# Feed-forward columns of both streams in one matmul, paired heads in part C, and a new order of the mixer's projections

## The chip, the core and the metric

The kernel runs on one core of a Trainium2 chip. Its engines are TensorE (PE; its weight loads are listed apart as PEld), VectorE (DVE), ScalarE (ACT), GpSimd (POOL) and SyncE (SP, which issues most loads). The metric is the device time of one execution in microseconds. Before the change the median of three runs is 2468.3 us (2467.7 to 2470.83).

## The reference, cut to what matters

Two transformer blocks of two layers each, in float32, 256 positions of width 1024. The first block (retention, stick-breaking attention, feed-forward) is left as it was but for buffers. The second carries two streams, the latents `x` and the context `h`, through the same weights:

```python
for l in range(DEPTH):                      # DEPTH = 2
    x = ffn_sublayer(x, mod_x, 0, *f0)      # swiglu, 1024 -> 2816 -> 1024
    h = ffn_sublayer(h, mod_h, 0, *f0)      # the same weights
    ax, ah = adaln_in(x, ...), adaln_in(h, ...)
    uv_x, qb_x, qc_x, kb_x, vb_x, kc_x, vc_x = split(ax @ w_in[l])
    # h: all of them in layer 0, only kb, vb, kc, vc in layer 1
    o_a = chunk_gmlp(uv_x, ...)             # part A: gelu, norm, 128 x 128 mix, times u
    o_b = diff_attention_latent(...)        # part B: 4 heads, two softmaxes of 64-wide keys each
    o_c = swa_latent(qc_x, kc_x, vc_x, kc_h, vc_h, sink)   # part C: 4 heads over 2 key-value heads
    x = adaln_out(x, concat(o_a, o_b, o_c) @ w_out[l], ...)
    # h the same in layer 0; then both through the second feed-forward
    x = ffn_sublayer(x, mod_x, 2, *f1)      # h too, but not in the last layer
```

`mod_x` and `mod_h` are products of a conditioning vector with `w_mod`, which is 9 x 1024 columns a layer.

## The kernel before, in words

**Precision.** A weight tile arrives as float32 (`raw`, four slots) and is split by ACT and DVE into a high and a low part (`hl`, five slots; a "granule" is one such tile of 512 KB). Activations are split in the same way (`y`, `a`, `o`). A product is three float32r matmuls, high by high, high by low and low by high (`mm3`). Attention itself runs in plain float32, where the program has two PE instructions for each matmul: the trace counts both, the order counts one.

**Feed-forward (`ffn`, `col`, `row_units`).** The 2816 hidden columns are 22 tiles `j`. A column (`col`) makes gate and up of tile `j` for one stream: 2 x 8 x 3 = 48 matmuls of 256 moving columns (the stream's 256 tokens) into one PSUM bank, tile `mm_c`; then ACT takes silu, DVE multiplies, ACT and DVE split the result into `a`. A row unit multiplies two tiles of `a` with one granule of the down weights, 6 matmuls of 512 columns; four make a row. The context H adds its rows up in SBUF (`mm_r`, `fo`), the latents X keep theirs in four PSUM banks (`mm_f`). Both streams use one granule of weights, so H and X stay within five granules of each other; X has granules of its own for its last two columns and rows (`OWN_C`, `OWN_R`), and in the second feed-forward of layer 0 for its first four columns (`OWN_B`).

**Mixer (`attn2`).** Projections are two half units of 24 matmuls each (`half1`, `half2`; `vb` is `wide1`, `wide2`) in the order kb0, kb1, vb, kcvc, v, qb0, u, qb1, qc. Softmax work is a list of items, eight for part B (head, half of the queries) and eight for part C; a stream of its own (`sat`) issues scores (`at_s`), softmax, transposes (`at_t`), weighted values (`at_o` in B, `at_c` in C), two items ahead (`DIST`). A B item has two score matmuls on the two halves of the partitions (64 rows of keys each); a C item has one. Part A's mix is `gm` (`at_g`), B's norm `bapply` (`st_rb`). Then `w_out` in four pieces, 1, 2 (B), 0 (A), 3 (C), 96 matmuls `mm_f<-hl,o`.

**Order.** `run` is a planner: it holds the streams `sx` (X), `sh` (H), `sat`, `smod` (the sums of `w_mod`, DVE work of the lowest class) and `stot`, knows a cost for each kind of unit (`PE_NS`, `BANKS`) and writes one fixed order of instructions for each engine. PSUM is eight banks. At run time only semaphores decide when the next instruction of that order starts. All line numbers in the trace are the helper's (L205), so groups are told apart by tile names: `mm_y` is the transposed input of a stage, `mm_t` the modulation sums, `st_*` norms.

Of the kernel before, what the change touches and what calls it, by code (L numbers as in the profile page):

```python
# [11 lines left out]
F32 = mybir.dt.float32  # L12
# [35 lines left out]
GM_AT = 11  # L48
# [75 lines left out]
class Gran:  # L124


    def __init__(self, ap, kind):
# [9 lines left out]
PE_NS = {"col": 5760, "proj": 5760, "rope1": 5760, "half1": 2880, "half2": 2880, "wide1": 5450, "wide2": 5450, "row": 1365, "row_add": 1365, "row_last": 1365,  # L137
         "tr": 450, "total": 440, "put": 110, "rbc": 430, "start1": 30, "start2": 300, "r1": 650, "r2": 650, "r3": 430,
         "hstat": 1650, "happly": 3400, "s1": 650, "s2": 870, "s3": 650, "rope2": 860, "kcvc2": 650, "wst": 430,
         "sc2": 1730, "sc1": 870, "trp": 430, "avf": 1300, "avc": 860, "bst": 320, "gm": 1040, "bapply": 1740}  # L140
BANKS = {"row": 0, "wide1": 2, "wide2": 0, "row_add": 1, "row_last": 0, "half2": 0, "happly": 2, "sc2": 2, "bapply": 2}
CLASS = {"part": 3, "head": CLS_H, "tr": CLS_T, "post": CLS_P, "row_last": CLS_R, "row_add": CLS_A, "rfac": CLS_F,
         **{k: CLS_S for k in ("tv", "sc1", "sc2", "trp", "avf", "avc", "bst")}}
# [24 lines left out]
class Engine:  # L168
# [6 lines left out]
    def ns(self, op, args, kw):  # L175
# [283 lines left out]
def tile_two_blocks(ctx: ExitStack, tc, io, out):  # L459
# [31 lines left out]

    ytile = [None, None]
# [3 lines left out]
    u_half = {}  # L496
    ctab = [None, None]
# [119 lines left out]
    def pre_units(st, c, gain_of, shift_of, of, deps, hard=False):  # L617
# [58 lines left out]
        for i in range(4):  # L676
            u = st.add("tr", tr(i), deps=d)
            d = ()
        return u

    def pre_raw(gain_of, deps_lo, deps_hi, keep, at_start=False):
# [145 lines left out]
    def ffn(st, c, gg, gu, gd, mode, dep, pace, fac=None, by_token=True):  # L827
        abox = {}
        cols = {}

        def col(j):
            def fn():
# [4 lines left out]
                def tail():  # L837
# [16 lines left out]
                    if j == 0:  # L854
# [237 lines left out]
    def block1_layer(l, dep):  # L1092
# [103 lines left out]
        for h in range(4):  # L1196
# [49 lines left out]
        for h in range(4):  # L1246
# [70 lines left out]
        def sapply():  # L1317
# [78 lines left out]
    def mod_buf1():  # L1396
        a = wk.tile([P, 2, 2, D], F32, tag="y1", name="modacc")
        r = [wk.tile([P, 2, D], F32, tag=t, name="modraw") for t in ("k2", "v2")]
        return [t[:, x, :] for t in r for x in range(2)], [[a[:, x, 0, :], a[:, x, 1, :]] for x in range(2)]

    def mod_buf2():
# [3 lines left out]
        a2 = [wk.tile([P, D], F32, tag="wt", name="modacc", bufs=2) for _ in range(2)]  # L1405
# [3 lines left out]
    mod_units(0, 2, 4, pace0[23], [(u_s2, 0.0)], mod_buf1)  # L1409
# [17 lines left out]
    ORDER = [5, 6, 7, 8, 9, 2, 3, 4, 1, 0]  # L1427

    def attn2(l, c, main, gw, kv_only, dep, kvdeps):
# [159 lines left out]
        roped("kb0", 5, lambda: K2["k"][:, 0:2, half], 1.0, 1, [dep] + ([(totals[l, 8], 0.0)] if c == H else kvdeps[:1]))  # L1589
        roped("kb1", 6, lambda: K2["k"][:, 2:4, half], 1.0, 1)  # L1590
        vb()
        kcvc()
        if kv_only:
            flush()
            return None, ev
        if c == H or l == DEPTH - 1:
# [20 lines left out]
        uvv()  # L1617
        roped("qb0", 2, lambda: B["q"][:, 0:2, :], 0.125, 1)
        uvu()
        roped("qb1", 3, lambda: B["q"][:, 2:4, :], 0.125, 1)  # L1620

        roped("qc", 4, lambda: B["qc"], 0.125, 1)
        flush()

# [6 lines left out]
        def soft(todo, extra=None):  # L1631
# [3 lines left out]
            for p, ps, x in todo:  # L1635
                V.tensor_reduce(x[:, 0:1], ps[:, :n], axis=AX.X, op=ALU.max, negate=True)
                if extra is not None:
                    V.scalar_tensor_tensor(x[:, 0:1], extra, -1.0, x[:, 0:1], op0=ALU.mult, op1=ALU.min)
            yield A
            for p, ps, x in todo:  # L1640
# [337 lines left out]
```

## Time and profile before

| | us |
|---|---|
| median of three runs (lowest, highest) | 2468.3 (2467.7, 2470.83) |
| profiled execution, its own time | 2468.97 |
| its span, first to last instruction | 2467.1 |
| PE busy | 2409.6 (98%) |
| DVE, ACT, POOL busy | 1727.6, 1094.3, 99.3 |
| mean granted TensorE clock | 0.993 of full |

The span has four kinds of stretch: block one up to about 660 us, then for each layer of block two a feed-forward of both streams (660 to 1050 and 1700 to 2090 us), the mixers (1050 to 1335 and 2100 to 2257 us), and a second feed-forward (1290 to 1710 us for both streams, 2270 to 2460 us for X alone). "Busy" of PE counts an instruction from its start to its modelled end, neighbours overlapping; the time that a matmul takes of PE in a stream is read from the starts of neighbours or from the chain.

### The profile page before, as it was taken

To read this page: it belongs to the slowest core of one execution; us is meant where nothing else is said; L and a number is where in the kernel's file an instruction comes from. 1 tells how busy PE (TensorE), PEld (TensorE's weight loads), DVE (VectorE), ACT (ScalarE), POOL (GpSimd) and SP (SyncE) were. 2 spreads that over 40 slices of the span, in tenths; PEclk is the share of its full clock that TensorE was granted. 3 is DMA by queue.
4 is the path that set the end of the run, shared out by engine and by line. 5 is a ranking of instruction groups with operands and counts; after the bars stand their busy time and mean duration, and the time that the engine had idled before them with its cause. 6 is when DMAs were issued, how large, how long until landed. Compare 5 with 4: busy or idle time off the path is not lost.

```text
span 2467.1 us, 41782 instructions
## 1 busy us (share of the span) xinstructions
PE 2409.6 (98%) x16543; PEld 2211.5 (90%) x16543; DVE 1727.6 (70%) x3366; ACT 1094.3 (44%) x2331; POOL 99.3 (4%) x189
## 2 busy tenths in 40 slices
PE   8999999999999999999999999999999999997998
PEld 7999999999999999989669999999999999866997
DVE  5789667798789933756688994348998448486554
ACT  6654456545532222636465222236322226465443
POOL 1000000010011000000000100000110000000000
PEclk9999999999999999999999999999999999999999
DMA  7568655686667533522226652245675335322663
GB/s 228 165 209 263 179 168 158 191 267 194 205 188 210 167 98 90 178 88 84 62 94 205 214 180 86 86 120 188 206 213 154 95 87 181 93 86 78 190 193 120
DMA packets 455301, 386.26 MB, mean 157 GB/s; under 512 B 20512, under 2 KB 380260, under 8 KB 455104
## 3 DMA queue, kind: packets, MB, share of 16 engines
q1 hardware_dynamic: 431280, 299.67, 41.0%
q0 software_dynamic: 23648, 83.77, 10.7%
q8 instruction: 130, 2.13, 0.4%
q14 instruction: 67, 0.55, 0.1%
q10 hardware_dynamic: 176, 0.14, 0.0%
HBM read 382.43 MB, written 1.10 MB: 155 GB/s over the span
## 4 chain that ended last, share of the span: by engine, by line
PE 88%; DVE 8%; ACT 1%; DMA 1%; issue 1%; DVEq 0%; ACTq 0%
PE mm_c L205 57%; PE mm_f L205 17%; PE mm_r L205 6%; DVE hl L205 2%; PE at_s L205 2%; PE mm_t L205 1%; DVE res L205 1%; PE at_o L205 1%; DVE fo L205 1%; PE at_t L205 1%; DMA raw<-in_w_in_dram 1%; DVE t L205 1%; PE at_c L205 1%; PE st_rb L205 1%; DVE rs_t L205 1%
## 5 line engine op out<-in xcount | busy, mean ns | idle before, releaser
L205 PE MATMUL mm_c<-y,hl 128*128 128x256 f32 x11616 | 1436.4, 284 | 10.4 <-DVE y L205 7.5
L205 PEld LDWEIGHTS mm_c<-y,hl 128*128 128x128 f32 x11616 | 1418.8, 192 | 23.8 <-DVE y L205 8.8
L205 ACT CAST hl<-raw 128x512 fp32r<-128x512 f32 x1128 | 649.0, 619 | 814.5 <-PE mm_c L205 445.3
L205 DVE TENSOR_TENSOR hl<-raw,hl 128x512 fp32r<-128x512 f32 x1128 | 733.2, 685 | 339.4 <-ACT hl L205 338.3
L205 PE MATMUL mm_f<-hl,a 128*128 128x512 f32 x1584 | 381.5, 393 | 0.0
L205 PEld LDWEIGHTS mm_f<-hl,a 128*128 128x128 f32 x1584 | 291.5, 188 | 57.6
L205 DVE SCALAR_TENSOR_TENSOR modacc<-modraw,sc,modacc 128x1024 f32<-128x1024 f32 x252 | 311.6, 1277 | 0.0
L205 ACT ACTIVATE sg<-mm_c 128x256 f32<-128x256 f32 x154 | 58.6, 381 | 311.0 <-PE mm_c L205 307.5
L205 PE MATMUL mm_r<-hl,a 128*128 128x512 f32 x792 | 190.5, 392 | 0.0
L205 DVE TENSOR_TENSOR sg<-sg,mm_c 128x256 f32<-128x256 f32 x154 | 64.0, 416 | 154.0 <-ACT sg L205 153.2
L205 PEld LDWEIGHTS mm_r<-hl,a 128*128 128x128 f32 x792 | 145.2, 188 | 28.0
L205 PE MATMUL mm_f<-hl,o 128*128 128x512 f32 x480 | 119.3, 399 | 0.0
L1000 POOL DMA_DIRECT2D modraw<-in_w_mod_dram x144 | 77.3, 538 | 991.6 <-DVE modacc L205 625.8
L205 PE MATMUL mm_c<-hl,y 128*128 128x512 f32 (+1 forms) x528 | 108.7, 363 | 0.0
L205 PEld LDWEIGHTS mm_f<-hl,o 128*128 128x128 f32 x480 | 87.8, 189 | 23.1 <-issue 4.6
L205 PEld LDWEIGHTS mm_c<-hl,y 128*128 128x128 f32 x528 | 88.8, 189 | 14.7 <-issue 0.3
L205 DVE TENSOR_TENSOR fo<-fo,mm_r 128x512 f32<-128x512 f32 x120 | 81.6, 682 | 9.2 <-PE mm_r L205 8.5
L205 ACT CAST a<-sg 128x256 fp32r<-128x256 f32 x154 | 62.5, 406 | 30.1 <-DVE sg L205 30.0
L205 DVE TENSOR_TENSOR a<-sg,a 128x256 fp32r<-128x256 f32 x154 | 64.4, 418 | 8.5 <-ACT a L205 8.5
L205 DVE TENSOR_TENSOR gu<-mm_c,rfac 128x512 f32<-128x512 f32 x44 | 30.3, 688 | 48.7 <-PE mm_c L205 48.6
L205 DVE TENSOR_REDUCE sx<-at_s 128x1 f32<-128x512 f32 (+1 forms) x72 | 40.8, 596 | 26.3 <-PE at_s L205 25.7
L205 DVE TENSOR_REDUCE modt<-mm_t 128x4 f32<-128x512 f32 x72 | 49.2, 684 | 8.4 <-PE mm_t L205 8.2
(196 smaller groups left out, 1412.4 us busy)
## 6 DMA issues: line engine op xcount, KB each, us to landing
modraw<-in_w_mod_dram POOLq DMA_DIRECT2D x144, 512.0 KB, 4.7
raw<-in_ffn_w_down_dram SPq DMA_DIRECT2D x100, 512.0 KB, 4.4
raw<-in_ffn_w_gate_dram SPq DMA_DIRECT2D x98, 512.0 KB, 4.7
raw<-in_ffn_w_up_dram SPq DMA_DIRECT2D x98, 512.0 KB, 3.9
raw<-in_w_in_dram SPq DMA_DIRECT2D x92, 512.0 KB, 4.7
raw<-in_w_gate_dram SPq DMA_DIRECT2D x44, 512.0 KB, 4.9
raw<-in_w_up_dram SPq DMA_DIRECT2D x44, 512.0 KB, 5.1
raw<-in_w_down_dram SPq DMA_DIRECT2D x44, 512.0 KB, 4.9
```

The costliest lines, as they stand in the source:

```text
L205: return f(*args, **kw)
L1000: G.dma_start(M["raw"][g % len(M["raw"])], wm[k * P:(k + 1) * P, i * D:(i + 1) * D])
```

## The change

1. **Joint columns.** `yy` is one buffer for the inputs of both streams. In a joint column one matmul has as its moving operand both streams' 256 tokens, `yy[:, :, 0, k, :]`, two runs of 256 columns that lie apart; gate and up are units of 24 matmuls with 512 columns, a bank each. ACT and DVE do silu and product once for 512 columns and the split into `a` once for each stream. Tiles 2 to 19 are joint in the first feed-forward of each layer and 4 to 19 in the second one of layer 0: 18 + 18 + 16 = 52 columns. The first joint gate also waits for X's input, and an up waits for the X row that last read the slots of `a` which it writes.
2. **Part C in pairs.** Eight items become four (query group, half of the queries), each with both key-value heads: two score matmuls on the two halves of the partitions, two softmaxes, eight transposes; the weighted values go to both halves of the output partitions, alternating. The rows of `w_out` for part C are loaded in a matching order, as two transfers of 64 partitions for a granule.
3. **Order.** The projections come as kb0, kb1, qb0, vb, qb1, kcvc, qc, v, u (layer 0) and kb0, kb1, vb, qb0, qb1, kcvc, qc, v, u (layer 1), `gm` after all items, `w_out` in pieces 1, 2, 3, 0. Scores wait only for the keys they use.
4. **Buffers.** `wt` has four buffers; the modulation sums of block one use the buffers that block two's used; the scratch for DMAs from GpSimd is set to 8192.

```diff
+BA_AT = 9
-GM_AT = 11
+GM_AT = (12, 12)
-PE_NS = {... "wide2": 5450, "row": 1365, ...}
+PE_NS = {... "wide2": 5450, "joint": 5450, "row": 1365, ... "trp2": 870, ...}
...
+    yy = cpool.tile([P, 2, 2, KT, S], F32R, name="yy")
-                    ytile[c] = wk.tile([P, 2, KT, S], F32R, tag=f"y{c}", name=f"y{c}")
+                    ytile[c] = yy[:, c]
...
+        def both(j):
+            box = {}
+
+            def part(g, ps):
+                for k in range(KT):
+                    mm3(ps, wsl(g, 0, k, 0, P), wsl(g, 1, k, 0, P), yy[:, :, 0, k, :], yy[:, :, 1, k, :],
+                        k == 0, k == KT - 1)
+
+            def gate():
+                ps = mm_ps([P, 2, S], "mm_c")
+                part(gg[j], ps)
+
+                def tail():
+                    yield A
+                    box["sg"] = t2k([P, 2, S], "sg")
+                    A.activation(box["sg"], ps, AF.Silu)
+                return tail
+
+            def up():
+                ps = mm_ps([P, 2, S], "mm_c")
+                part(gu[j], ps)
+
+                def tail():
+                    yield V, ug
+                    sg = box["sg"]
+                    V.tensor_mul(sg, sg, ps)
+                    for x in (H, X):
+                        yield A
+                        a = joint[1]["a", x]
...
+                        hl = a["t"][:, j % 4]
+                        A.copy(hl[:, 0, :], sg[:, x, :])
+                        yield V
+                        V.tensor_sub(hl[:, 1, :], sg[:, x, :], hl[:, 0, :])
+                        a[j] = hl
+                return tail
+            ug = st.add("joint", gate, grans=[gg[j]], deps=dep if j == 0 else ())
+            cols[j] = joint[1][j] = st.add("joint", up, grans=[gu[j]])
...
         for j in range(NJ):
-            col(j)
+            if joint is None or j not in joint[0]:
+                col(j)
+            elif c == H:
+                both(j)
+            else:
+                cols[j] = joint[1][j]
+                if j == joint[0][0]:
+                    joint[1]["first"].deps += ((last_of[X], 0.0),)
             if j >= 3 and j % 2 == 1:
-                row(j // 2 - 1)
+                u = row(j // 2 - 1)
+                if joint and c == X and j + 1 in joint[0]:
+                    joint[1][j + 1].deps += ((u, 0.0),)
...
-    mod_units(0, 0, 2, pace0[1], [(u_s2, 0.0)], mod_buf1)
+    mod_units(0, 0, 2, pace0[1], [(u_s2, 0.0)], mod_buf2)
...
+    SEQ = ("kb0 kb1 qb0 vb qb1 kcvc qc v u".split(),
+           "kb0 kb1 vb qb0 qb1 kcvc qc v u".split())
...
-        for v in range(2):
-            for g in range(2):
-                for b in range(2):
-                    hh = v * 2 + g
-
-                    def sc(v=v, g=g, b=b, hh=hh):
-                        ps = at_ps([P, 512], "at_s")
-                        PE.matmul(ps[:, :n], B["qc"][v * 64:v * 64 + 64, g, b * P:(b + 1) * P],
+        for g in range(2):
+            for b in range(2):
+                def sc(g=g, b=b):
+                    pt = ptile()
+                    pss = [at_ps([P, 512], "at_s") for _ in range(2)]
+                    for v in range(2):
+                        PE.matmul(pss[v][:, :n], B["qc"][v * 64:v * 64 + 64, g, b * P:(b + 1) * P],
                                   K2["kc"][v * 64:v * 64 + 64, 0:n], start=True, stop=True)
...
+                def avc(g=g):
+                    ps = at_ps([P, 512], "at_c")
+                    for j in range(nk):
+                        for v in range(2):
+                            PE.matmul(ps[v * 64:v * 64 + 64, :S], K2["vc"][:, j, v * 64:v * 64 + 64],
+                                      B["wtc", g][v][:, j, :], start=(j == 0), stop=(j == nk - 1))
...
-            otile[c] = wk.tile([P, 2, KT, S], F32R, tag=f"y{c}", name=f"o{c}")
+            otile[c] = yy[:, H] if l == DEPTH - 1 else yy[:, c]
...
+        pieces = (1, 2, 3, 0) if GM_AT[l] >= 12 else (1, 2, 0, 3)
+        joints = [(range(n, NJ - OWN_C), {}) for n in (2, OWN_B)]
...
+    nc = _bacc.Bacc("TRN2", target_bir_lowering=False, num_devices=1,
+                     dynamic_dma_scratch_size=8192)
```

What stands on PE in the first feed-forward of layer 0, before (`y_6515` is H's input, `y_7250` X's; `a_7247` and `a_7420` are their hidden tiles):

```order
L205 MATMUL mm_f<-hl,a_7420 128x512 x18
L205 MATMUL mm_c<-y_6515,hl 128x256 x48
L205 MATMUL mm_r<-hl,a_7247 128x512 x12
L205 MATMUL mm_c<-y_7250,hl 128x256 x96
L205 MATMUL mm_r<-hl,a_7247 128x512 x12
L205 MATMUL mm_f<-hl,a_7420 128x512 x6
L205 MATMUL mm_c<-y_6515,hl 128x256 x48
L205 MATMUL mm_f<-hl,a_7420 128x512 x18
L205 MATMUL mm_c<-y_6515,hl 128x256 x48
L205 MATMUL mm_r<-hl,a_7247 128x512 x12
```

And after, over the same tiles (`a_7395` is X's):

```order
L206 MATMUL mm_f<-hl,a_7395 128x512 x24
L206 MATMUL mm_c<-yy,hl 128x512 x72
L206 MATMUL mm_r<-hl,a_7247 128x512 x24
L206 MATMUL mm_c<-yy,hl 128x512 x24
L206 MATMUL mm_f<-hl,a_7395 128x512 x24
L206 MATMUL mm_c<-yy,hl 128x512 x72
L206 MATMUL mm_r<-hl,a_7247 128x512 x24
L206 MATMUL mm_c<-yy,hl 128x512 x24
L206 MATMUL mm_f<-hl,a_7395 128x512 x24
```

Each `mm_c` of 48 with 256 columns for either stream has gone into a `mm_c` of 24 with 512 for both, and H's and X's rows stand whole between them.

PE around the first scores of X in the mixer of layer 1, before (`at_s<-k` scores of part B, `at_r` rotations):

```order
L205 MATMUL mm_c<-y_21857,hl 128x256 x96
L205 MATMUL at_r<-kr,tab_c_6411 128x256 x2
L205 MATMUL mm_c<-y_21857,hl 128x256 x24
L205 MATMUL at_s<-k_21693,at_21912 128x512 x4
L205 MATMUL mm_c<-y_21857,hl 128x256 x48
L205 MATMUL at_s<-k_21693,at_21912 128x512 x2
L205 MATMUL at_t<-cst,p 128x128 x4
L205 MATMUL at_s<-k_21693,at_21912 128x512 x2
L205 MATMUL mm_c<-y_21857,hl 128x256 x24
L205 MATMUL at_t<-cst,p 128x128 x4
```

And after:

```order
L206 MATMUL mm_c<-yy,hl 128x256 x144
L206 MATMUL at_t<-cst,kcr 128x128 x2
L206 MATMUL at_r<-kr,tab_c_6412 128x256 x2
L206 MATMUL mm_c<-yy,hl 128x256 x24
L206 MATMUL at_s<-k_19011,at_19237 128x512 x4
L206 MATMUL mm_c<-yy,hl 128x256 x24
L206 MATMUL at_r<-kr,tab_c_6412 128x256 x2
L206 MATMUL at_s<-k_19011,at_19237 128x512 x2
L206 MATMUL mm_c<-yy,hl 128x256 x24
L206 MATMUL at_t<-cst,p 128x128 x4
L206 MATMUL at_s<-k_19011,at_19237 128x512 x2
L206 MATMUL mm_c<-yy,hl 128x256 x24
```

The first scores stand further ahead: before, 48 + 24 projection matmuls of X are still to come behind them, now seven half units of 24.

PE at the end of the same mixer, before (`at_s<-kc` scores of part C, `at_c` its weighted values, `at_g` part A, `mm_f<-hl,o` the product with `w_out`):

```order
L205 MATMUL at_s<-kc,at_21912 128x512
L205 MATMUL at_t<-cst,p 128x128 x4
L205 MATMUL at_c<-wtc,vc 64x256 x4
L205 MATMUL at_s<-kc,at_21912 128x512
L205 MATMUL at_t<-cst,p 128x128 x4
L205 MATMUL mm_f<-hl,o_23026 128x512 x12
L205 MATMUL at_t<-cst,p 128x128 x4
L205 MATMUL at_c<-wtc,vc 64x256 x4
L205 MATMUL at_t<-cst,p 128x128 x4
L205 MATMUL mm_f<-hl,o_23026 128x512 x6
L205 MATMUL at_c<-wtc,vc 64x256 x4
L205 MATMUL mm_f<-hl,o_23026 128x512 x78
```

And after (`mm_f<-hl,yy` is that product, since `o` lies in `yy`):

```order
L206 MATMUL at_s<-kc,at_19237 128x512 x2
L206 MATMUL at_t<-cst,p 128x128 x8
L206 MATMUL st_h<-cst,bq 128x1 x2
L206 MATMUL st_rb<-cst,rs_t 128x128 x8
L206 MATMUL at_t<-cst,p 128x128 x8
L206 MATMUL at_c<-wtc,vc 64x256 x8
L206 MATMUL at_t<-cst,p 128x128 x8
L206 MATMUL at_c<-wtc,vc 64x256 x8
L206 MATMUL at_g<-ws,bt_19238 64x128 x8
L206 MATMUL mm_f<-hl,yy 128x512 x96
```

The scores of C stand in pairs, `at_c` in groups of eight, `at_g` behind all of them, and the whole product with `w_out` behind `at_g`, where 18 of its 96 matmuls stood between the last items.

## Rows read from the trace of the kernel before

**Rows 1.** The page, part 1: span and busy time of each engine.
```profile
span 2467.1 us, 41782 instructions
...
PE 2409.6 (98%) x16543; PEld 2211.5 (90%) x16543; DVE 1727.6 (70%) x3366; ACT 1094.3 (44%) x2331; POOL 99.3 (4%) x189
```

**Rows 2.** The page, part 4: chain that ended last, by engine.
```profile
PE 88%; DVE 8%; ACT 1%; DMA 1%; issue 1%; DVEq 0%; ACTq 0%
```

**Rows 3.** Chain of waits, 840 to 960 us: start us, length us, what.
```profile
848.11 5.47 PE mm_r L205 x24
...
897.90 11.51 PE mm_c L205 x96
```

**Rows 4.** Timeline of PE, layer 1 mixer: start us, us, what [idle before].
```profile
2178.66 1.13 PE L205 MATMUL at_s<-k,at 64*128 64x512 f32 x4
2179.72 0.66 PE L205 MATMUL at_t<-cst,p 128*128 128x128 f32 x4
...
2208.97 1.12 PE L205 MATMUL at_s<-kc,at 64*128 64x512 f32 x2
2210.02 0.66 PE L205 MATMUL at_t<-cst,p 128*128 128x128 f32 x4
...
2216.21 1.94 PE L205 MATMUL at_c<-wtc,vc 128*64 128x256 f32 x8
2218.08 1.12 PE L205 MATMUL at_s<-kc,at 64*128 64x512 f32 x2
...
2219.63 1.95 PE L205 MATMUL st_rb<-cst,rs_t 128*128 128x128 f32 x16
2221.51 1.09 PE L205 MATMUL at_g<-ws,bt 128*64 128x128 f32 x16
2222.53 1.12 PE L205 MATMUL at_s<-kc,at 64*128 64x512 f32 x2
2225.87 0.63 PE L205 MATMUL at_t<-cst,p 128*128 128x128 f32 x4 [2.22 <-DVE p L205]
...
2238.83 17.97 PE L205 MATMUL mm_f<-hl,o 128*128 128x512 f32 x78
```

**Rows 5.** Timeline of PE, layer 0 mixer of the context stream.
```profile
1153.64 0.70 PE L205 MATMUL at_s<-k,at 64*128 64x256 f32 x4
1154.28 0.44 PE L205 MATMUL at_t<-cst,p 128*128 128x128 f32 x2
...
1178.36 0.70 PE L205 MATMUL at_s<-kc,at 64*128 64x256 f32 x2
1178.98 0.44 PE L205 MATMUL at_t<-cst,p 128*128 128x128 f32 x2
...
1191.22 1.08 PE L205 MATMUL at_c<-wtc,vc 128*64 128x256 f32 x4
1192.23 0.70 PE L205 MATMUL at_s<-kc,at 64*128 64x256 f32 x2
```

**Rows 6.** Three stretches: busy us of each engine, clock, DMA share, GB/s.
```profile
core 0: us, PE busy (x) PEld busy (x) DVE busy (x) ACT busy (x) POOL busy (x), PEclk, DMA share, GB/s
750.00:800.00 50.00, 50.00 (x348) 46.51 (x347) 48.58 (x75) 13.21 (x30) 7.49 (x13) 1.00 0.73 219
1065.00:1335.00 270.00, 258.50 (x1602) 211.95 (x1603) 179.34 (x477) 152.30 (x358) 3.70 (x7) 0.98 0.32 95
2101.00:2257.00 156.00, 148.39 (x877) 119.29 (x877) 98.13 (x229) 77.55 (x171) 0.00 (x0) 0.99 0.31 90
```

**Rows 7.** The page, part 5: DVE's modulation sums.
```profile
L205 DVE SCALAR_TENSOR_TENSOR modacc<-modraw,sc,modacc 128x1024 f32<-128x1024 f32 x252 | 311.6, 1277 | 0.0
```

**Rows 8.** Groups of instructions by shape: ACT's table loads.
```profile
L205 ACT ACT_TABLE_LOAD x34 | 43.6, 1283 | 2.2 <-PEq L1966 1.7
```

**Rows 9.** The page, part 6: DMA issues of the modulation weights.
```profile
modraw<-in_w_mod_dram POOLq DMA_DIRECT2D x144, 512.0 KB, 4.7
```

More of the change, by code (lines that the diff above doesn't have):

```diff
@@ L676, in pre_units @@
         for i in range(4):
[L677 removed]
+            u = last_of[c] = st.add("tr", tr(i), deps=d)
             d = ()
@@ L825, in row_units, with ffn @@
         return u
-    def ffn(st, c, gg, gu, gd, mode, dep, pace, fac=None, by_token=True):
-        abox = {}
+    def ffn(st, c, gg, gu, gd, mode, dep, pace, fac=None, by_token=True, joint=None):
+        abox = joint[1].setdefault(("a", c), {}) if joint else {}
         cols = {}
+        def both(j):
[22 more added lines that the diff above has]
+                        a = joint[1]["a", x]
+                        if "t" not in a:
+                            a["t"] = wk.tile([P, 4, 2, S], F32R, tag=f"B{x}", name=f"a{x}")
+                        hl = a["t"][:, j % 4]
[7 more added lines that the diff above has]
+            if j == joint[0][0]:
+                joint[1]["first"] = ug
+            pace.append(cols[j])
         def col(j):
@@ L1587, in uvu @@
             step("u", tail, 0)
[L1589 to L1596, printed above, removed]
+        if not kv_only and (c == H or l == DEPTH - 1):
             def layer_consts():
@@ L1616, in attn2 @@
             late.append(lambda: main.add("wst", wst))
[L1617 to L1622, printed above, removed]
+        first = [dep] + ([(totals[l, 8], 0.0)] if c == H else kvdeps[:1])
+        make = {"kb0": lambda: roped("kb0", 5, lambda: K2["k"][:, 0:2, half], 1.0, 1, first),
+                "kb1": lambda: roped("kb1", 6, lambda: K2["k"][:, 2:4, half], 1.0, 1),
+                "vb": vb, "kcvc": kcvc, "v": uvv, "u": uvu,
+                "qb0": lambda: roped("qb0", 2, lambda: B["q"][:, 0:2, :], 0.125, 1),
+                "qb1": lambda: roped("qb1", 3, lambda: B["q"][:, 2:4, :], 0.125, 1),
+                "qc": lambda: roped("qc", 4, lambda: B["qc"], 0.125, 1)}
+        for name in SEQ[l]:
+            if not kv_only or name in ("kb0", "kb1", "vb", "kcvc"):
+                make[name]()
         flush()
+        if kv_only:
+            return None, ev
         def ptile():
@@ L1808, in attn2 @@
                 add_sc(i + DIST)
-            tu = sat.add("trp", items[i][3][1], deps=[(tv, 0.0)])
+            tu = sat.add("trp" if i < 8 else "trp2", items[i][3][1], deps=[(tv, 0.0)])
             todo, post = post, []
@@ L1875, in tile_two_blocks @@
         go = [load_rows(io["w_out_2"][l], 4) for _ in range(2)]
+        for gp in go:
+            gp[3] = [Gran([io["w_out_2"][l][768 + P * v:768 + P * (v + 1), 512 * e:512 * (e + 1)].rearrange(
+                "(k p) n -> p k n", p=64) for v in range(2)], "row") for e in range(2)]
         f1 = (load_m(io["ffn_w_gate_2"][l, 1], NJ), load_m(io["ffn_w_up_2"][l, 1], NJ),
@@ L1887, in tile_two_blocks @@
             coef_unit(main, l, c, 0)
-            u = ffn(main, c, *ff[c][0], mode, [(u, L_TR)] + (dep[1] if c == H and l == 0 else []), pace.setdefault((l, c, 0), []))
+            u = ffn(main, c, *ff[c][0], mode, [(u, L_TR)] + (dep[1] if c == H and l == 0 else []), pace.setdefault((l, c, 0), []),
+                    joint=joints[0])
             if c == H:
@@ L1909, in tile_two_blocks @@
             coef_unit(main, l, c, 2)
-            u = ffn(main, c, *ff[c][1], "ps" if last else mode, [(u, L_TR)], pace.setdefault((l, c, 1), []))
+            u = ffn(main, c, *ff[c][1], "ps" if last else mode, [(u, L_TR)], pace.setdefault((l, c, 1), []),
+                    joint=None if last else joints[1])
             cur[c] = post_units(main, c, "ps" if last else mode, u, last, last, last)
@@ L1931, in load @@
             for e, ap in enumerate(g.ap):
-                nc.sync.dma_start(rv[:, :, 64 * e:64 * e + 64], ap)
+                half = slice(64 * e, 64 * e + 64)
+                nc.sync.dma_start(rv[half] if g.kind == "row" else rv[:, :, half], ap)
         else:
```

131 lines of the change are left out of this document (70 added, 61 removed).

## The prediction

> **What bounds the kernel now.** I read the page's busy shares first. PE is busy for 2409.6 of 2467.1 us [rows 1], so no more than 57.5 us are idle on PE, and an edit that saves more than that must make PE's own work shorter. The chain of waits says the same: 88% of the span is PE, 8% is DVE [rows 2]. Then I split the span. In the stretch from 750 to 800 us, the first feed-forward of layer 0, PE shows 50.00 us of 50 at a granted clock of 1.00, 2.4 GHz [rows 6]: a microsecond less of matmul there is a microsecond less of time, as long as nothing else runs out. DVE nearly does, at 48.58 of 50. The two mixers are looser: PE has 11.50 us idle in the 270 us of layer 0's mixers and 7.61 us in the 156 us of layer 1's, at a clock of 0.98 and 0.99 [rows 6]. Their idle time is in short waits for softmax work on DVE, such as 2.22 us ahead of a transpose [rows 4]. So the sum is one of PE's matmul time, stage by stage, and then of those 19.1 us.
>
> **Joint columns.** The chain gives both prices in a full stream. Two columns, 96 matmuls with 256 columns, take 11.51 us, 119.9 ns each; 24 matmuls with 512 columns take 5.47 us, 227.9 ns each [rows 3]. 256 and 512 columns at 2.4 GHz are 106.7 and 213.3 ns, so either shape pays 13 to 15 ns on top, and the wide one pays it half as often. A tile j costs 11.51 us now (one column for H, one for X) and 2 x 5.47 = 10.94 us joint: 0.57 us less. 52 joint tiles give 29.6 us. The joint moving operand is in two runs of 256 columns with a gap between them; no matmul of this trace reads such an operand, so 227.9 ns is the price of a contiguous one. The bounds are therefore 0 (each run priced as a matmul of 256, 239.8 ns) and 29.6 us; I take 29.6, since what is halved is the number of instructions.
>
> The Trainium skill has another price (TensorE: Matmul & The Clock Gate, section Back-to-back issue gap): a warm matmul takes N / 2.4 ns and a fixed 2.5 ns. By that a pair of 256s and a 512 would differ by 2.5 ns, a tile by 0.12 us, and 52 tiles by 6.2 us; that is an estimate from the page alone. The 119.9 ns in the chain disagree with its 109.2 ns for 256 columns, so the sum goes by the rows.
>
> ACT and DVE do silu and product for 512 columns in one instruction in place of two and the same splits; that takes work off them, not on. The new waits: X's input before the first joint gate is waited for by X's own columns now, behind the same H columns (two in a first feed-forward, four in layer 0's second), and in the order the X row that frees slots of `a` stands on PE ahead of the up that waits for it. I cost both at nothing; their cover is that PE reaches them in this order anyway.
>
> **Part C in pairs.** B's scores are pairs of 64-row matmuls already: a pair (x4 in the trace) holds PE from 2178.66 to 2179.72, 1.06 us; a single C score (x2) from 2208.97 to 2210.02, 1.05 us [rows 4]. Two halves of the array thus run beside each other. X has 8 singles a layer, 8.40 us, and gets 4 pairs, 4.24: 4.16 us less, twice. H has half the keys: single 0.62, pair 0.64 us [rows 5], 8 x 0.62 - 4 x 0.64 = 2.4 us less, once. Together 10.7 us.
>
> The weighted values (`at_c`, 64 output columns of the array) take 1.87 us for four matmuls in X [rows 4] and 1.01 us for two in H [rows 5]. Alternating the output halves should let them overlap. The nearest row is part A's mix, eight matmuls of 128 columns on alternating halves in 1.02 us (2221.51 to 2222.53), against eight of full width in 1.88 us (2219.63 to 2221.51) [rows 4]: a ratio of 0.54. Eight paired `at_c` are then 2 x 1.87 x 0.54 = 2.02 us, a layer of X 4.04 in place of 7.48, twice, and H 2.18 in place of 4.04: 6.9 + 1.9 = 8.7 us. Bounds: 0 (no overlap) and 9.5 (full); I take 8.7.
>
> DVE and ACT have as many instructions for C as before. The transposes are the same number.
>
> **Order of the mixer.** This adds no matmul and removes none, so it can only fill the idle 19.1 us or add to them. In layer 1, where no other stream works, four half units of projection (96 matmuls, 11.5 us at 119.9 ns) move from ahead of the first scores to behind them, beside B's softmax, where PE waits now. Against that, the 18 `w_out` matmuls that stood between the last items (4.1 us at 227.9 ns) go behind `at_g`: 96 follow there in one run, before that 78 in 17.97 us [rows 4]. Putting gelu last makes ACT change its table more often in that mixer: in ACT's order 6 loads in place of 3, at 1283 ns [rows 8], 3.8 us of ACT in the middle of the exponentials; in layer 0 it is 4 in place of 9. `bapply` of layer 0 now waits for the last projection, as it shares `yy` with the input; behind it in the attention's stream stand only part C's last items and the product with `w_out`. I take a quarter of the 19.1 us as regained, 4.8 us. Bounds: all 19.1 regained, or 19.4 us (10.7 + 8.7) of C's gain lost to new waits.
>
> **Edits at nothing.** Block one's modulation sums change buffers, not number. Four loads are kept in flight as before; each lands in 4.7 us [rows 9] and feeds two parts of 1277 ns, before which DVE never waits [rows 7]. If the smaller scratch allowed only two in flight, one would still come every 2.35 us for 2.55 us of work. The six granules of `w_out` that now come in two transfers meet a DMA share of 0.31 to 0.32 in the mixers [rows 6].
>
> **Sum.** 29.6 + 10.7 + 8.7 + 4.8 = 53.8 us. The profiled execution took 2468.97 us, 1.87 above its span and 0.67 above the median of the runs: 2468.97 - 53.8 = 2415.2, on the median 2414.5. I say 2415.
>
> **Rivals.**
>
> *Joint columns gain nothing* (two runs cost two matmuls): 2415 + 29.6 = 2445 us. For it: no such operand in the trace. Against it: weight loads and instructions are halved whatever the reader of the operand does. By the page's fixed cost, as above, it would be 2438 us; that goes with this rival.
>
> *The mixers give their gain back.* DVE, not PE, sets the pace there: in layer 1 it is busy 98.1 of 156 us [rows 6], and in a pair of C items every DVE step still comes twice in a row before PE can go on, with nothing but 12 or so `w_out` matmuls beside it. Then 10.7 + 8.7 + 4.8 us turn into waits and 29.6 us remain: 2439 us.
>
> *Slower: DVE holds joint columns up where the modulation sums run.* A joint column fills two banks at once; four are X's rows, so the next gate, up and row share what is left, and each bank comes free only through ACT or DVE. DVE runs at 48.58 of 50 us there [rows 6], in strict order, and one part of the sums is 1277 ns [rows 7]. If PE waits for one part at each joint column, 52 x 1.28 = 66 us are lost and the time is 2415 + 66 = 2481 us. The change stops paying at 53.8 / 52 = 1.03 us a column. Against it: PE lost nothing in the same stretch at the same load of DVE, and the sums run beside only a part of the 52.
>
> *No change* needs the first two together, 2468.97 less some 5 us, or less.
>
> **How the numbers follow.** Forecast 0.67, of which a few in 100 are cases better than it; mixers give back 0.14; joint columns gain nothing or little 0.11; both 0.04; slower 0.04. The likeliest is 2415. Its own range, with `at_c` and the idle time at their bounds, is 2400 (9.5 and 19.1 in place of 8.7 and 4.8) to 2424 (`at_c` at 0). For 8 in 10 I cut a little off the low end and take in the mixers' rival: 2402 to 2440. About 0.2% (5 us) is what a measurement of this kernel can tell from no change; faster by more than that 0.92, within it 0.04, slower 0.04.
>
> **What would show it.** In the changed profile: a joint half of 24 matmuls at 5.47 us in the chain (5.75 is the first rival); `mm_c` of 256 columns down to 6624, 2496 of 512 new. Pairs of C scores at 1.06 us, eight `at_c` at about 2.0 us (3.7: no overlap). PE idle in the two mixer stretches at 19 us or below; above 35 us the second rival is true. In the first feed-forwards PE at 50 of 50 us still; if waits for DVE stand ahead of `mm_c` there, the slower rival is at work. The prediction is wrong if the time is above 2440 us, or if it falls below 2400, where the order of the mixer would be worth more than all the idle time that I gave it.

## The result, and the profile after

The changed kernel takes 2402.31 us (median of 4 runs, 2401.14 to 2405.21) against 2469.57 us in the same session: ratio 0.973, 95% interval 0.9713 to 0.9747, 67 us less. The forecast was 2415 and its range 2402 to 2440, so the time lies inside the range by 0.3 us, less than the runs differ among themselves: that it falls just inside and not just outside is chance. Joint columns and pairs worked as forecast; one term, the order of the mixer, was far too small, and what bounded it left a cost out.

The page of the kernel after, parts 1 and 4, against [rows 1, 2]:

```profile
span 2401.3 us, 36659 instructions
...
PE 2353.5 (98%) x14047; PEld 2072.4 (86%) x14047; DVE 1719.0 (72%) x3314; ACT 1081.1 (45%) x2271; POOL 103.8 (4%) x189
...
PE 88%; DVE 8%; ACT 1%; issue 1%; DMA 1%; DVEq 0%; ACTq 0%
```

PE is still the bound. Its busy time fell by 56.1 us and its idle time from 57.5 to 47.8. To place this, I cut both spans where PE waits for a new stage's input (its first `mm_c` behind a wait for `y`, in the latents; the last cut is where PE's transposes wait for `z`, the input of the last feed-forward). All in us, by one profiled execution each:

| | block one | ff 1, layer 0 | mixers, layer 0 | ff 2, layer 0 | ff 1, layer 1 | mixers, layer 1 | last ff, end |
|---|---|---|---|---|---|---|---|
| before | 675.9 | 389.1 | 269.2 | 378.4 | 389.2 | 165.5 | 199.8 |
| after | 677.1 | 377.9 | 242.8 | 367.2 | 379.4 | 156.9 | 200.1 |
| forecast of the gain | 0 | 10.3 | 14.8 | 9.1 | 10.3 | 9.5 | 0 |
| gain | -1.2 | 11.2 | 26.4 | 11.2 | 9.8 | 8.6 | -0.3 |

(Block one lies between 675.7 and 678.7 in all fourteen profiles, with old and new buffers; its 1.2 us tell nothing. The forecast's row is its own terms, split by stage.)

The joint columns in the chain of waits of the kernel after (start us, length us), against [rows 3]:

```profile
900.16 16.32 PE mm_c L206 x72
916.48 5.44 PE mm_r L206 x24
921.92 5.44 PE mm_c L206 x24
```

24 matmuls of 512 columns take 5.44 us, 226.7 ns each, two runs of 256 or not. A joint tile is 10.88 us where two columns were 11.51.

The stretches of [rows 6] in the kernel after (busy us of each engine, granted clock, DMA share, GB/s):

```profile
750.00:800.00 50.00, 50.00 (x234) 41.27 (x233) 49.79 (x73) 13.31 (x26) 8.10 (x13) 1.00 0.70 216
1054.00:1298.00 244.00, 239.27 (x1596) 204.24 (x1597) 176.23 (x479) 143.43 (x349) 3.86 (x7) 1.00 0.35 104
2044.00:2191.00 147.00, 142.11 (x877) 118.80 (x877) 96.45 (x228) 79.60 (x171) 0.00 (x0) 0.98 0.32 94
```

In this stretch of the feed-forward PE has no idle time although DVE is at 49.79 of 50 us. In layer 1's first feed-forward PE does wait once for a modulation sum, which the kernel before does not:

```profile
1711.72 0.66 PE L206 MATMUL mm_t<-cst,modacc 128*128 128x128 f32 x4 [1.06 <-DVE modacc L206]
```

In layer 0's mixers idle time fell from 11.50 to 4.73 us and the mean clock is 1.00, not 0.98. Of the 4.73, 0.9 stand ahead of the table's cut and 3.2 are the wait for the next stage's input, so hardly any wait is left inside. In layer 1 4.89 us are left, from 7.61. What is left there stands in PE's timeline (start us, us, what [idle before]), against [rows 4]:

```profile
2137.04 1.13 PE L206 MATMUL at_s<-kc,at 64*128 64x512 f32 x4
2138.10 3.14 PE L206 MATMUL mm_c<-yy,hl 128*128 128x256 f32 x24
...
2148.23 1.90 PE L206 MATMUL at_t<-cst,p 128*128 128x128 f32 x8 [1.28 <-DVE p L206]
...
2157.64 2.95 PE L206 MATMUL st_rb<-cst,rs_t 128*128 128x128 f32 x16 [2.49 <-DVE rs_t L206]
2160.38 1.83 PE L206 MATMUL at_t<-cst,p 128*128 128x128 f32 x8
2162.15 1.95 PE L206 MATMUL at_c<-wtc,vc 128*64 128x256 f32 x16
2164.03 1.09 PE L206 MATMUL at_t<-cst,p 128*128 128x128 f32 x8
...
2167.20 0.38 PE L206 MATMUL at_g<-ws,bt 128*64 128x128 f32 x2
2167.41 0.38 PE L206 MATMUL at_c<-wtc,vc 128*64 128x256 f32 x1
```

A pair of C scores holds PE for 1.06 us (2137.04 to 2138.10), eight paired `at_c` for 1.88 (2162.15 to 2164.03): what four took before. Behind the wait of 2.49 us `st_rb` takes 2.95 us, against 1.95 in [rows 4]: the granted clock is 0.65 from 2158 to 2160 us and 0.50, the lower level of 1.2 GHz, from 2160 to 2162. Not every such wait has this behind it: after the 2.22 us in [rows 4] the clock stayed at 1.00, and the next group took its usual time:

```profile
2226.43 1.94 PE L205 MATMUL at_c<-wtc,vc 128*64 128x256 f32 x8
```

### The profile page after: what moved, and what is told of

Read it like the earlier page. It is cut to its first block, busy times and chain, and to the rows that moved or that the text cites. A ratio compares the mean times of both kernels' runs of the same rounds, so it can differ in the third digit from the quotient of the medians.

```text
span 2401.3 us, 36659 instructions
## 1 busy us (share of the span) xinstructions
PE 2353.5 (98%) x14047; PEld 2072.4 (86%) x14047; DVE 1719.0 (72%) x3314; ACT 1081.1 (45%) x2271; POOL 103.8 (4%) x189
## 4 chain that ended last, share of the span: by engine, by line
PE 88%; DVE 8%; ACT 1%; issue 1%; DMA 1%; DVEq 0%; ACTq 0%
PE mm_c L206 57%; PE mm_f L206 17%; PE mm_r L206 6%; DVE hl L206 2%; PE at_s L206 1%; PE mm_t L206 1%; PE at_o L206 1%; DVE fo L206 1%; DVE res L206 1%; PE at_t L206 1%; DVE t L206 1%; PE st_rb L206 1%; DMA raw<-in_w_in_dram 1%; DVE modacc L206 1%; DVE rs_t L206 1%
## 5 line engine op out<-in xcount | busy, mean ns | idle before, releaser
L206 PE MATMUL mm_c<-yy,hl 128*128 128x256 f32 (+1 forms) x9120 | 1405.8, 314 | 10.5 <-DVE yy L206 7.5
L206 PEld LDWEIGHTS mm_c<-yy,hl 128*128 128x128 f32 x9120 | 1276.9, 192 | 117.8 <-DVE yy L206 8.9
L206 PE MATMUL mm_f<-hl,a 128*128 128x512 f32 x1584 | 379.4, 393 | 0.0
L206 PE MATMUL mm_r<-hl,a 128*128 128x512 f32 x792 | 184.9, 390 | 0.0
L206 ACT ACTIVATE sg<-mm_c 128x256 f32<-128x256 f32 (+1 forms) x102 | 50.0, 490 | 255.5 <-PE mm_c L206 251.7
L206 DVE TENSOR_TENSOR sg<-sg,mm_c 128x256 f32<-128x256 f32 (+1 forms) x102 | 56.4, 553 | 119.0 <-PE mm_c L206 96.1
L206 PE MATMUL mm_f<-hl,yy 128*128 128x512 f32 x480 | 117.5, 397 | 0.0
L206 PE MATMUL mm_c<-hl,yy 128*128 128x512 f32 (+1 forms) x528 | 109.4, 364 | 0.0
L206 PEld LDWEIGHTS mm_f<-hl,yy 128*128 128x128 f32 x480 | 88.0, 188 | 20.8 <-issue 1.9
L206 PEld LDWEIGHTS mm_c<-hl,yy 128*128 128x128 f32 x528 | 89.0, 189 | 15.2 <-issue 0.7
L206 ACT CAST a<-sg 128x256 fp32r<-128x256 f32 x154 | 57.6, 404 | 32.3 <-DVE sg L206 32.0
L206 DVE TENSOR_REDUCE modt<-mm_t 128x4 f32<-128x512 f32 x72 | 49.3, 685 | 19.1 <-PE mm_t L206 18.9
```

The costliest lines, as they stand in the source:

```text
L206: return f(*args, **kw)
```

## The experiments

Every time is a median against `before` in the same session (2468.7 to 2469.6 us); differences to `after` are to its 2402.31.

**No joint columns.**

```diff
-        joints = [(range(n, NJ - OWN_C), {}) for n in (2, OWN_B)]
+        joints = [None, None]
```

> The kernel after with no joint columns: every column is a column of one stream again, 256 wide. Theory A (the gain of a joint tile is the issue gap paid half as often; the two traces give 11.51 and 10.88 us for a tile, 0.63 us each): 52 x 0.63 = 33 us slower than after, 2435 us, with columns at 11.51 us per 96 matmuls in the chain and no new waits. Theory B (forecast's size, 0.57 us a tile): 29.6 us, 2432. Rival (a shared input also keeps the two streams in step and so took waits out of the feed-forwards): 38 us or more, with new idle time of PE in the feed-forwards.

Measured 2436.37 us, ratio 0.9864 (0.985 to 0.9877): 34.1 us slower than after. The three stages with joint columns grew by 11.5, 11.0 and 9.6 us, 32.1 in all; the mixers moved by -0.1 and +1.0. The chain of waits of this kernel:

```profile
891.67 5.75 PE mm_c L206 x48
897.42 2.75 PE mm_f L206 x12
900.17 11.51 PE mm_c L206 x96
```

It has the tile's 11.51 us back, and no new wait; the wait of 1.06 us for `modacc` is gone with the joint columns. Theory A holds, 0.62 us a tile; the forecast's 0.57 priced a 512 at 227.9 ns and not at 226.7. (Rows broken into twelves cost 2.75 us, 5.50 for 24, so whole rows are a little cheaper too.)

**The gap in the moving operand.**

```diff
-    yy = cpool.tile([P, 2, 2, KT, S], F32R, name="yy")
+    yy = cpool.tile([P, 2, KT, 2, S], F32R, name="yy")
...
-                    mm3(ps, wsl(g, 0, k, 0, P), wsl(g, 1, k, 0, P), yy[:, :, 0, k, :], yy[:, :, 1, k, :],
+                    mm3(ps, wsl(g, 0, k, 0, P), wsl(g, 1, k, 0, P), yy[:, 0, k], yy[:, 1, k],
...
```

> The kernel after with the shared input laid out so that both streams' 256 tokens of one k are neighbours: the moving operand of a joint column is one run of 512 columns. Theory A (PE's time does not depend on the gap): within 3 us of after, 24 matmuls at 5.44 us. Rival 1 (two runs cost something, hidden in the 226.7 ns): faster by 1 ns a matmul or more, 2.5 us and up. Rival 2 (the input of one stream, now 256 columns a row of 512, is slower to write or to read for ACT and DVE): slower by 2 us or more.

Measured 2403.41 us, ratio 0.974 (0.9727 to 0.9754); 1.1 us above after, within what can be told. Its chain:

```profile
900.26 16.32 PE mm_c L206 x72
```

72 matmuls take 16.32 us in either kernel, 226.7 ns each. Two runs of 256 columns cost what one of 512 costs.

**Part C in single items.** Eight items with one score matmul, and weighted values of one head at a time.

```diff
-        for g in range(2):
-            for b in range(2):
-                def sc(g=g, b=b):
+        for g in range(2):
+            for v in range(2):
+                for b in range(2):
+                    def sc(v=v, g=g, b=b):
...
-BA_AT = 9
-GM_AT = (12, 12)
+BA_AT = 11
+GM_AT = (16, 16)
...
```

> The kernel after with part C's items single again (eight items, one score matmul each, weighted values of one head at a time), all else as after. Theory A (pairs are worth the overlap on the array and no more): scores 16 x 1.05 - 8 x 1.06 + 8 x 0.62 - 4 x 0.64 = 10.7 us and weighted values 9.5 us, 20 us slower than after, 2422, and no idle time comes back in layer 0's mixer. Rival (the pairs took the waits of before out of the mixers): 20 us and most of 13.7 us of idle time and low clock, 32 to 34 us, 2435. Rival the other way (the order's filler hides part of it): under 15 us.

Measured 2420.67 us, ratio 0.9802 (0.9789 to 0.9815): 18.4 us slower. The mixers are 257.4 and 161.7 us, 14.6 and 4.8 longer, 19.4 together, the forecast's 10.7 + 8.7. That the sum agrees to the tenth is chance: by layer the forecast was 11.9 and 7.6. The waits stay out of layer 0 (PE has 5.43 us idle in 258 us, clock 1.00), so the pairs are not what removed them. In layer 1 only 4.8 of the 7.6 us forecast are there: with singles PE waits less for `st_rb` (0.9 us, after: 2.5), and that group takes 2.02 us, not 2.95.

**Weighted values by head, not alternating.**

```diff
-                    for j in range(nk):
-                        for v in range(2):
+                    for v in range(2):
+                        for j in range(nk):
```

> The kernel after with the eight matmuls of a pair's weighted values ordered by head: four to the one half of the output partitions, then four to the other, in place of alternating. Theory A (neighbours on different halves overlap, in full): X's groups go from 1.88 to 3.74 us and H's from 1.02 to 2.03: 4 x 1.87 + 2 x 1.01 = 9.5 us slower, 2412. Rival (other work or waits set the end there): 0 to 4 us, since a wait for softmax behind the group shrinks by as much.

Measured 2404.82 us, ratio 0.9737 (0.9724 to 0.975): 2.5 us slower, not 9.5. Not because something hid it: the context's groups did not become longer, and the latents' by half of what theory A said. PE's timeline of this kernel, first the context, then the latents:

```profile
1177.10 1.09 PE L206 MATMUL at_c<-wtc,vc 128*64 128x256 f32 x8
1178.12 1.13 PE L206 MATMUL at_r<-kr,tab_c 128*128 128x256 f32 x4
...
1241.09 2.86 PE L206 MATMUL at_c<-wtc,vc 128*64 128x256 f32 x16 [0.29 <-ACT wtc L206]
1243.88 1.09 PE L206 MATMUL at_t<-cst,p 128*128 128x128 f32 x8
```

The context's group takes 1.02 us in either order, the latents' 2.79 against 1.88 alternating and 3.74 in sequence (two times the 1.87 of [rows 4]). Four groups of 0.91 us more are 3.6 us, and the mixers' stages grew by 3.4. Work on the other half starts even when some instructions of the first half stand ahead of it. In the latents' group each half has eight instructions, two for each of its four matmuls; by their starts in the trace the second half's first starts at 1242.01 us, together with the first half's fifth. The kernel after shows the same at 2167.20 us above: two instructions of `at_g` start ahead of the last one of `at_c`, which the written order has before them. So most of the gain of pairing is in issuing both heads in one unit; alternation is worth the rest. Theory A missed that, and the rival's 0 to 4 us covers the number for another reason.

**The order of before, with pairs and joint columns.**

```diff
-    SEQ = ("kb0 kb1 qb0 vb qb1 kcvc qc v u".split(),
-           "kb0 kb1 vb qb0 qb1 kcvc qc v u".split())
+    SEQ = ("kb0 kb1 vb kcvc v qb0 u qb1 qc".split(),
+           "kb0 kb1 vb kcvc v qb0 u qb1 qc".split())
-GM_AT = (12, 12)
+GM_AT = (9, 9)
```

> The kernel after with the projections in the order of before (kb0 kb1 vb kcvc v qb0 u qb1 qc), gm beside the second pair of part C and the pieces 1, 2, 0, 3. Theory A (the order is what took the waits and the half-speed matmuls out of layer 0's mixer, 7.7 us of idle time and some 6 us of low clock by the two traces): 12 to 15 us slower than after, about 2416, with waits for softmax work near the end of H's and X's mixer in layer 0 and a granted clock below 1.00 there. Theory B (forecast's size of the order): about 5 us, 2407. Rival (the waits went because pairs halve the number of softmax hand-overs): 0 to 3 us.

Measured 2431.1 us, ratio 0.9844 (0.983 to 0.9857): 28.8 us slower, twice what my largest theory said. Mixers 264.4 and 164.7 us; of the 21.6 us in layer 0, 15.4 are idle time of PE and the rest is busy time. PE's longest wait, and DVE in the same stretch:

```profile
1249.49 1.09 PE L206 MATMUL at_g<-ws,bt 128*64 128x128 f32 x16
1258.04 1.94 PE L206 MATMUL at_t<-cst,p 128*128 128x128 f32 x8 [7.46 <-DVE sx L206]
```

```profile
1249.99 0.74 DVE L206 SCALAR_TENSOR_TENSOR bt<-bt,subg,st_rb 128x512 f32<-128x512 f32 x1
...
1252.07 0.68 DVE L206 TENSOR_TENSOR yy<-bt,yy 128x512 fp32r<-128x512 f32 x1
...
1253.78 2.73 DVE L206 SCALAR_TENSOR_TENSOR res<-mm_f,rs_t,res 128x512 f32<-128x512 f32 x4
1256.42 0.68 DVE L206 TENSOR_TENSOR yy<-bt,yy 128x512 fp32r<-128x512 f32 x1
1257.02 0.15 DVE L206 TENSOR_TENSOR sx<-sx 128x1 f32<-128x1 f32 x1
1257.21 0.16 DVE L206 RECIPROCAL sx<-sx 128x1 f32<-128x1 f32 x1
1257.41 0.49 DVE L206 TENSOR_SCALAR p<-p,sx 128x512 f32<-128x512 f32 x1
```

DVE is not idle; it does part B's norm, splits, and the context's residual, and 0.8 us of softmax that PE needs stand behind them. PE has by then used up the context's `w_out`, which is what could have stood beside that.

**The two halves of the order.** Only `SEQ` as in the diff above, or only `GM_AT = (9, 9)` with the pieces 1, 2, 0, 3.

> The kernel after with only the projections in the order of before (kb0 kb1 vb kcvc v qb0 u qb1 qc in both layers); gm stays behind all items and the pieces 1, 2, 3, 0. It splits the 28.8 us of old_order. Theory A (the order of the projections: with v and u early, the context's part B starts late and no projection is left to stand beside part C's softmax): 15 to 25 us slower than after, with waits for part B's norm and for part C's softmax of several us in layer 0. Theory B (gm and its two DVE steps and split in the middle of part C): 0 to 8 us.

> The kernel after with only gm moved back beside the second pair of part C and the pieces of w_out back to 1, 2, 0, 3; the projections in the order of after. Theory A (the order of the projections carries the 28.8 us): 0 to 8 us slower than after. Theory B (gm's place): 15 us or more, with part C's transposes waiting for DVE behind gm's adds and split. A third way: faster than after by 1 to 3 us in layer 1, where 18 of the w_out matmuls could again stand between the last pairs.

Measured 2416.93 us (ratio 0.9791, 0.9778 to 0.9804) and 2420.68 (0.9804, 0.9791 to 0.9818): 14.6 and 18.4 us slower; mixers 253.1 and 159.7, 256.1 and 160.2. Each half alone costs half or more of the 28.8 us, and the two add to 33.0: they overlap, and a theory that gives all to one is wrong. PE's longest waits in layer 0 are 5.83 us ahead of `st_rb` with the old projections, and 4.63 us ahead of a pair's transposes with `gm` in part C.

**Joint columns alone**: single items, the order of before, gm and `bapply` at item 11, the rest as after.

> The joint columns and buffers of after, with part C in single items, the projections in the order of before, gm at the fourth single item of part C and the pieces 1, 2, 0, 3. Theory A (the terms are separate stages, the joint columns worth 33 to 34 us): 2469.6 - 33.5 = 2436 us; then pairs are worth 5 us in the old order (old_order is 2431) and 18 in the new one, and the order 15 us with singles and 29 with pairs. Rival (singles in the old order lose more with shared buffers, as the norm of part B waits for the last projection): 2445 or more.

Measured 2443.22 us, ratio 0.9897 (0.9884 to 0.9911). The feed-forwards gained 11.3, 9.8 and 11.1 us, 32.2 in all, as in after. The mixers are 271.4 and 169.7 us, 2.2 and 4.2 longer than before. So something else in the change (shared buffers, dependencies of scores and `bapply`, or only where the planner puts DVE's steps) costs the old order 6.4 us. Which edit it is was not tried and stays open, as do pairs alone in the kernel before. By mixers, pairs are worth 12.0 us in the old order (441.1 to 429.1) and 19.4 in the new one, the order 22.0 us with singles and 29.4 with pairs.

**The order alone**, in the kernel before, in layer 0 only.

```diff
+    SEQ = ("kb0 kb1 qb0 vb qb1 kcvc qc v u".split(), ...)
...
+        pieces = (1, 2, 3, 0) if l == 0 else (1, 2, 0, 3)
...
+        if l == 0:
+            ug = sat.add("gm", gm, deps=[(ev["v"], 0.0), (ev["u"], 0.0), (uba, 0.0)])
```

> The kernel before with only layer 0's mixers in the new order: projections kb0 kb1 qb0 vb qb1 kcvc qc v u, gm behind all items, w_out in pieces 1, 2, 3, 0; single items, single columns, layer 1 as before. Theory A (the order gives DVE's softmax chain projections and w_out to stand beside, so the waits of 3.4, 2.8 and 2.1 us go with the slow stretches behind them): mixer of layer 0 from 269.2 to 256 to 260 us, kernel 2457 to 2460. Theory B (forecast's size, a quarter of the idle time): 265 to 267 us, 2466. Rival (the order pays only together with pairs and four buffers for the transposed weights): 268 us or more.

Measured 2457.98 us, ratio 0.9951 (0.9937 to 0.9964), 10.8 us faster than before; mixers of layer 0 269.2 to 256.4 us, 12.8 less, as theory A had it. It still has two buffers for the transposed weights and no pairs, so the order does not need them. PE in the context's part C before:

```profile
1196.71 3.65 PE L205 MATMUL st_rb<-cst,rs_t 128*128 128x128 f32 x16 [3.42 <-DVE rs_t L205]
...
1203.77 0.66 PE L205 MATMUL at_t<-cst,p 128*128 128x128 f32 x2 [1.75 <-DVE p L205]
```

The stretch of layer 0's mixers in this kernel (as in [rows 6]), and PE's timeline in the context's part C:

```profile
1065.00:1325.00 260.00, 255.49 (x1613) 211.54 (x1614) 179.33 (x480) 151.49 (x360) 3.67 (x7) 1.00 0.33 98
```

```profile
1188.42 1.95 PE L205 MATMUL st_rb<-cst,rs_t 128*128 128x128 f32 x16
...
1194.03 3.11 PE L205 MATMUL mm_c<-y,hl 128*128 128x256 f32 x24
1196.97 0.38 PE L205 MATMUL at_t<-cst,p 128*128 128x128 f32 x2
1197.29 1.08 PE L205 MATMUL at_c<-wtc,vc 128*64 128x256 f32 x4
1198.29 3.14 PE L205 MATMUL mm_c<-y,hl 128*128 128x256 f32 x24
```

Projections now stand where before PE waited 3.42 us for `rs_t` and 1.75 us for `p` (1193 to 1204 us there); 4.5 us are idle in place of 11.5, and the clock is 1.00. Cut as in the table, PE's idle time fell from 11.5 to 3.5 us, of which 3.2 are the wait for the next stage's input, and its busy time from 257.7 to 252.9. The matmuls are the same ones, so 8.0 us of the gain are waits and 4.8 us are matmuls that ran at half speed before. This is the term that the forecast had at 2.9 us for this layer.

**Waits filled with dummy matmuls**, first in the kernel before. They write to a bank that is overwritten next; PE's order is otherwise unchanged.

```diff
+    def warm(ps, n):
+        for _ in range(n):
+            nc.tensor.matmul(ps, ident, cst[:, :S], start=True, stop=True)
...
```

> The kernel before with constant 128x128 by 128x256 matmuls, whose results are overwritten, in three of PE's waits of layer 0's mixers: 7 ahead of the context's st_rb (waits 3.42 us), 3 ahead of its transposes behind at_g (1.75) and 4 ahead of the latents' (2.15). One costs about 0.45 us by at_o (eight halves in 1.82 us), so 3.2, 1.4 and 1.8 us, a little less than each wait. Theory A (the matmuls behind such a wait run at half speed because PE stood still; 0.82, 0.80 and 0.82 of the clock in three stretches of 9 us): no such stretch any more and 4 to 6 us less, mixer of layer 0 from 269.2 to 264 us, kernel 2464. Rival (the clock is low there for another reason, or the waits set all of the time): mixer within 1 us of 269.2. Rival the other way (the added matmuls push DVE's work back): slower by 1 to 5 us.

Measured 2469.02 us, ratio 1.0 (0.9991 to 1.0009); mixers of layer 0 266.6 us, 2.6 less. The two stretches of low clock in before, and the latents' wait there (PE busy us, clock, DMA share, GB/s; then the timeline):

```profile
1191.00:1209.00 18.00, 12.83 (x60) 0.81 0.10 30
1272.00:1281.00 9.00, 8.55 (x32) 0.82 0.92 305
```

```profile
1271.09 0.63 PE L205 MATMUL at_t<-cst,p 128*128 128x128 f32 x4 [2.15 <-DVE rs_t L205]
1271.65 3.50 PE L205 MATMUL at_c<-wtc,vc 128*64 128x256 f32 x8
```

And the stretches that answer to them in this kernel:

```profile
1192.00:1210.00 18.00, 16.76 (x91) 1.00 0.10 30
1272.00:1281.00 9.00, 6.96 (x30) 1.00 0.89 299
```

```profile
1197.72 2.05 PE L205 MATMUL st_rb<-cst,rs_t 128*128 128x128 f32 x16 [0.32 <-DVE rs_t L205]
...
1203.84 0.44 PE L205 MATMUL at_t<-cst,p 128*128 128x128 f32 x2 [0.93 <-DVE p L205]
...
1277.30 0.66 PE L205 MATMUL at_t<-cst,p 128*128 128x128 f32 x4 [1.06 <-DVE p L205]
```

The slow stretches are gone (`st_rb` 2.05 us in place of 3.65), so the low clock did come of PE's standing still in these places. The time followed only in part: of the 4.8 us that half speed cost by `order_alone`, the stage got 2.6 back, and the kernel nothing that can be told (0.5 us, where the interval is about 2 us either way). For the rest PE now waits for DVE a little later, so DVE's chain set the end there and PE's half speed lay beside it. The order gave more: it takes the waits themselves away.

> The kernel after with the same kind of added matmuls in its three long waits: 20 ahead of the transposes of the last feed-forward's input (10.51 us of wait), 5 ahead of layer 1's st_rb (2.49 us), 6 ahead of the first column of the latents' second feed-forward in layer 0 (3.20 us). Theory A (half speed follows PE's standing still): the stretch from the last transposes to the end 200.1 to 197 us, the mixer of layer 1 156.9 to 155, 4 to 6 us in all, about 2397. Rival (no effect of a wait but its own length): within 1 us of after, 2402.

The same in the kernel after: 2400.41 us, ratio 0.9725 (0.9712 to 0.9738), 1.9 us less than after, which can't be told from none; theory A had 4 to 6. Mixers of layer 1: 155.0 us, 1.9 less, as theory A had it there. The other two places gave nothing that can be told; in the last one the twenty dummies ended too early:

```profile
2190.42 8.80 PE L592 MATMUL mm_y<-cst 128*128 128x256 f32 x40
2201.00 3.23 PE L206 MATMUL mm_y<-cst,z 128*128 128x128 f32 x16 [1.79 <-DVE z L206]
```

It is the lowest median of all kernels here.

**Three items ahead** (`DIST = 3`).

> The kernel after with softmax items three ahead in place of two. Theory A (what is left of waits in layer 1's mixer, 1.28 and 2.49 us, is the depth of the pipeline of items): mixer of layer 1 2 to 4 us shorter, 2399. Rival (DVE's order holds it up, scores earlier only bring more DVE work ahead of the old items): same or slower by up to 10 us in the mixers.

Measured 2411.93 us, ratio 0.9771 (0.9757 to 0.9784), 9.6 us slower than after; mixers 249.8 and 159.0 us. PE's waits in layer 1's (us in total, times, longest):

```profile
PE st_rb L206 <- DVE sx L206: 2.3, 1, 2.3
PE at_s L206 <- DVE at L206: 2.1, 1, 2.1
PE at_t L206 <- DVE sx L206: 1.8, 2, 1.3
```

They only moved: depth is not what is short. The rival's size is right (layer 0's mixers grew by 7.0 us, 3.9 of them idle time of PE); that DVE's order is the reason, as it says, was not shown.

## Why the prediction came out as it did

- **PE as the bound, and its time per tile**: right. Joint columns gave 32.1 us where 29.6 were forecast; the term is short by the 1.2 ns between 227.9 and 226.7. "I take 29.6, since what is halved is the number of instructions" is borne out by `no_joint` and `contiguous`. The rival that they gain nothing fell, and with it the 6.2 us that follow from the Trainium skill (TensorE: Matmul & The Clock Gate, section Back-to-back issue gap): this trace again has 13 ns on top of 512 columns.
- **Part C**: scores and weighted values 19.4 us forecast, 19.4 in `single_c`, with 2.7 us too little in layer 0 and 2.8 too much in layer 1, which cancel. The ratio 0.54 was a little cautious (eight `at_c` 1.88 us, not 2.02), and "alternating the output halves should let them overlap" named too narrow a condition.
- **Order of the mixer**: the step that failed is "I take a quarter of the 19.1 us as regained, 4.8 us", and with it that the order "can only fill the idle 19.1 us". Alone, in layer 0, it gave 12.8 us, more than all the 11.50 us idle there, of which 4.5 remain. Cut as in the table, 8.0 us of idle time were regained, where a quarter was 2.9, and 4.8 us came from PE's busy time: matmuls at 1.2 GHz behind the waits, such as `st_rb` at 3.65 us. I had read the clock of 0.98 in [rows 6] and not priced it. `before_filled` shows that the 4.8 can't simply be added either: with the clock kept up and the order as before, 2.6 of them came back. In layer 1 the order was not run by itself.
- In layer 0 the parts close: 6.6 us of scores, 5.7 of `at_c` (11.5 us of PE before, four groups of 1.88, 1.88, 1.02 and 1.02 after) and 12.8 for the order are 25.1 of the 26.4 us. The split depends on where one starts: undone from the kernel after, the order is worth 21.6 us there (`old_order`). In layer 1 the forecast's 9.5 became 8.6. PE's idle time fell by 2.7 us ([rows 6] against the kernel after), but its busy time only by 6.3 (148.39 to 142.11), less than the 7.9 us of scores and `at_c` that pairs take away: the mean clock fell from 0.99 to 0.98, with half-speed matmuls such as `st_rb` at 2.95 us. So a part of the pairs' gain came back, as the second rival had it, on a small scale.
- **Slower rival** (DVE holds joint columns up): DVE went from 48.58 to 49.79 of 50 us in that stretch and PE lost nothing. With DVE that full the margin is small, and in layer 1's first feed-forward it was used up once: 1.06 us of waiting for `modacc`. Such a wait stands in eight of the ten traces with joint columns and in none of the four without. The rival had that loss at each of 52 columns.
- **Edits at nothing**: no term of them shows in the kernel after. In the old order the rest of the change cost 6.4 us (`joint_alone`), which I had not foreseen.

## What to carry to other kernels

Where PE waits for short vector steps, look at what matmul work is still unissued at that moment, and order the independent matmuls so that some is left for the end; here that was worth 12.8 us in one layer by itself, and more than the overlap on the array when undone from the kernel after (29.4 us of mixers against 19.4). Read the granted clock beside the idle time when such waits are priced, then test whether the vector chain or PE sets the end before the two are added. Combine streams that share weights into one wide moving operand: here it saved some 13 ns for each instruction less, in stages where PE was all but never idle, and it did not depend on the operand lying in one piece.

## What was not expected of the hardware

Groups on the two halves of the array overlap without alternating instruction by instruction: two matmuls on one half and then two on the other take 1.02 us, as alternating; four and four take 2.79 us, between 1.88 and 3.74. An instruction on one half can start ahead of earlier ones on the other. Filling waits of 3.42, 1.75 and 2.15 us with matmuls kept the clock at 1.00 and saved 2.6 us in the stage and nothing measurable in the kernel.
